# Values of an RWKV-7 layer: one transposed copy of off-head rows, and copies moved from ScalarE to GpSimd and VectorE

## The chip, the cores and the metric

The kernel runs on one core of a Trainium2 chip. Its engines are named as in the profile: PE (TensorE, matrix multiplication and transposes), PEld (its weight loads), DVE (VectorE), ACT (ScalarE), POOL (GpSimd) and SP (SyncE, which here issues the loads of weights). Each engine works through its own instructions in order, and engines wait for each other by semaphores. The metric is the device time of one execution in microseconds; shorter is better.

## The reference

One block of a streaming encoder on 256 tokens of width 2048, in float32: an RMSNorm, one input projection, two mixers in parallel (RWKV-7 with 16 heads of 64, and a latent attention), gates, an output projection, a feed-forward part with a convolution, and a per-layer embedding. The change touches the RWKV-7 recurrence alone. For each head it keeps a 64 x 64 state and runs over the tokens:

```python
def step(state, inp):
    r_t, w_t, k_t, v_t, kk_t, a_t = inp
    sa = jnp.einsum('bhvk,bhk->bhv', state, -kk_t)
    state = (state * w_t[:, :, None, :]
             + sa[..., None] * (kk_t * a_t)[:, :, None, :]
             + v_t[..., None] * k_t[:, :, None, :])
    y_t = jnp.einsum('bhvk,bhk->bhv', state, r_t)
    return state, y_t
```

Before it, r, k and v come out of the projection (mixed with the token before), the decay w and the rate a out of small low-rank products, and kk is the normalised key. After it the output is normalised per head, a bonus term (r k r_k) v is added, and a gate multiplies.

## The kernel before

**The whole.** All weights stream from HBM in pieces of 128 x 1024 float32 (tile `raw`). Each half of a piece is split into a rounded part `hi` (an ACT cast, L148) and a remainder `lo` (a DVE subtraction, L149), and each product is made of three fast matmuls (L183 to L185 in `fm3`: hi by hi, hi by remainder, `lo` by hi). There are 5 buffers each for `hi` and `lo`, and 3 for `raw`. This stream of dense matmuls goes on through the whole kernel.

**The RWKV stage.** Two heads make a pair j: 128 channels on the 128 partitions, head 0 on partitions 0 to 63 and head 1 on 64 to 127. Two pairs run side by side (`par` 0 and 1), and four such double pairs, which this text calls turns, follow each other. `rw_pair` (L714) is a generator that yields between its steps. The loop at L1045 advances the current turn, the prologue of the next one and the epilogue of the last one, and after each step lets the dense work go on by so many matmul groups. In the machine code this makes blocks of 12, 18 or 30 dense matmuls on PE between the steps of the recurrence. A scheduler then sets the order on each engine by priorities and its own estimate of times; that order is fixed when the kernel is built, and each engine keeps to it.

**One turn.** The recurrence is worked in four chunks of 64 tokens.

- *Prologue* (L728 to L808): decays (`ld`, `cs`, `pp`, `pin`), normalised keys (`kk`, whose squares `sq` go to PE at L767 as `pq`), then `kr` (keys and receptances, scaled) and `bk` (columns 0 to 63 the beta keys, 64 to 127 the k' keys, and for head 1 once more the beta keys in 128 to 191, L799, so that each head finds its two blocks side by side).
- *Inverse* (L811 to L904): products `pg` (L820), masked into `gm`, and the inverse of a 64 x 64 triangular matrix per chunk and head: blocks of 16 by substitution on DVE (L848 to L859), then to 32 by two rounds of small matmuls, `ph` and `px` (L889 to L894), then to 64 (L897 to L903). `Y` and `H`, halves of the tile `YH`, hold the transposed inverse and the product between. The finished inverse lies in `Xb`: its two diagonal blocks of 32 are copied per partition quarter by ACT (L914, four copies a pair), the off-diagonal ones come from `px` (L902 on ACT, L903 on DVE).
- *Turned keys* (L906 to L912): `pb` holds the transposed keys of one head, in PSUM, and ACT copies it into `bt`, once per head.
- *Values* (L916 to L930): see below.
- *Chunk loop* (L934 to L955), for each chunk: `pc` = gm by sv (L939); its two heads' blocks are copied into `R` (L940 on ACT, L941 on DVE); Xb by R (L943); the result, negated, goes into the own-head blocks of `av` (L944 on ACT, L945 on DVE); bt by av (L952) and the decayed state `s0` (L949, ACT) give the next chunk's state in `sv` (L954, DVE).
- *Epilogue* (L957 to L999): the outputs `yc` from kb by sv and gm by av, the norm, bonus, gate, and a split into `yrw` (L161, L162).

**How sv and av are laid out.** Both are [128, 4 chunks, 2 halves, 64]. In sv, partitions of head h hold in half h the state of that head (64 key channels by 64 value channels), and in the other half the values of a chunk, turned (64 tokens by 64 value channels). So for head 0 the values stand on partitions 64 to 127, for head 1 on partitions 0 to 63, and one matmul with a 128-row contraction takes state and values in one go. av has the same off-head blocks; its own-head blocks are written in the chunk loop.

Before the change PE transposes v in blocks of 128 tokens that start at tokens 0, 64 and 128, and a fourth from `vw`, a small tile that GpSimd fills with tokens 192 to 255 and 0 to 63 (L784, L785). By this shift both heads' values land on the partitions where they belong, but as pieces that have to be put in place: three ACT copies into sv and the same three into av (L924 to L926), of 64 partitions each. GpSimd clears the two own-head blocks of sv's first chunk (L930).

**Tiles and buffers.** In the RWKV stage `e1` gives tiles of 128 x 256 from 7 buffers per parity, `e2` tiles of 128 x 512 from 3. PSUM has two small buffers per parity (`small`). A tile's first writer waits until the last reader of the tile that held the buffer is done.

Of the kernel before, what the change touches and what calls it, by code (L numbers as in the profile page):

```python
# [12 lines left out]
ALU = mybir.AluOpType  # L13
# [95 lines left out]
def hybrid_block(tc, A):  # L109
# [604 lines left out]
    def rw_pair(J, j, k, r, v):  # L714
# [11 lines left out]
        c4 = lambda ap: ap.rearrange("p (c n) -> p c n", c=NCH)  # L726

# [55 lines left out]
        vw = ep.tile([P, 2, C], F32, name=f"vw{par}", bufs=1)  # L783
        nc.gpsimd.tensor_copy(vw[:, 0, :], v[:, 3 * C:4 * C])  # L784
        nc.gpsimd.tensor_copy(vw[:, 1, :], v[:, 0:C])  # L785
# [13 lines left out]
        act(bk[64:128, :, 2 * C:3 * C], bk[64:128, :, 0:C], AF.Copy)  # L799
# [28 lines left out]
        yield NONE, STEP  # L828

# [41 lines left out]
        heads = ((0, slice(0, 64)), (1, slice(64, 128)))  # L871
# [11 lines left out]
        YH = e2("YH")  # L883
# [6 lines left out]
        tt(out=H, in0=ph, in1=K("lm", 0, 32).unsqueeze(1).to_broadcast([P, NCH, 32]), op=ALU.mult)  # L890
        yield NONE, STEP
        px = each("px", own, lambda i, c: H[Q[i], c, :], Xc)
        tt(out=Xc[:], in0=Xc[:], in1=px, op=ALU.subtract)
        nc.vector.transpose(out=Y, in_=Xc[:])  # L894
# [3 lines left out]
        act(H[Q[1]], ph[Q[1]], AF.Copy)  # L898
        nc.vector.tensor_copy(H[Q[3]], ph[Q[3]])
# [7 lines left out]
        for h in range(2):  # L907
            hs = slice(64 * h, 64 * h + 64)
            pb = small("pb")
            for c in range(NCH):  # L910
                nc.tensor.transpose(pb[:, c * C:c * C + C], bk[hs, c, h * C:h * C + 2 * C], ident[hs, hs])
            act(bt[:, :, h, :], pb[:, 0:T].rearrange("p (c n) -> p c n", c=NCH), AF.Copy)  # L912
        for i in range(4):
            act(Xb[Q[i], :, i // 2, i % 2 * 32:i % 2 * 32 + 32], Xc[Q[i]], AF.Copy)  # L914
# [4 lines left out]
        for c in range(3):  # L919
            nc.tensor.transpose(pv[:, c * P:c * P + P], v[:, c * C:c * C + P], ident)  # L920
        nc.tensor.transpose(pv[:, 3 * P:4 * P], vw[:].rearrange("p a n -> p (a n)"), ident)
        p4 = pv[:].rearrange("p (c n) -> p c n", c=NCH)
        for dst in (sv, av):
            act(dst[0:64, :, 1, :], p4[0:64, :, C:P], AF.Copy)  # L924
            act(dst[64:128, 1:4, 0, :], p4[64:128, 0:3, 0:C], AF.Copy)
            act(dst[64:128, 0, 0, :], p4[64:128, 3, 0:C], AF.Copy)  # L926
        R = ep.tile([P, C], F32, name=f"R{par}", bufs=1)
        lo_, hi_ = slice(0, 64), slice(64, 128)
        for h, hs in heads:
            nc.gpsimd.memset(sv[hs, 0, h, :], 0.0)  # L930
        two = lambda ap: ap.rearrange("p h n -> p (h n)")
# [513 lines left out]
```

## Time and profile before

| | before |
|---|---|
| median of 3 runs | 1575.75 us (1575.26 to 1576.95) |
| the profiled execution | 1574.22 us |
| its span, first to last instruction | 1572.4 us |
| mean granted clock of PE | 0.996 |
| busy in the span: PE, DVE, ACT, POOL | 1544.4, 1178.2, 966.1, 29.7 us |
| the RWKV stage | about 180 to 600 us of the span |

The page gives busy times, a map of the span in 40 slices, the chain of work that ended last, and the costliest groups of instructions. In a group's row stand source line, engine, operation, written and read tiles, shape and count; then busy time and mean; then the idle time of the engine just before these instructions, with what ended it. In the view of waits a row names the engine and line that waited, what released it, the total in us, the number of times and the longest. In the view of stretches a row gives busy time and number of instructions of each engine, the clock that PE was granted (1.00 is full speed), the busy share of the DMA engines, and GB/s. The view of one line gives minimum, median and longest duration in ns. In the timeline a row begins with the start and the duration in us; in square brackets stands the idle time before it.

The clock of PE can be lower than full speed for a few microseconds, and a PE that runs slowly counts as busy all the same. Matmuls overlap, so a row's duration is more than the time that one of them adds.

### The profile page before, as it was taken

How to read it: one execution, taken by the hardware profiler on the slowest of the kernel's cores; microseconds unless marked ns; L12 is line 12 of the kernel's file. 1: busy time of each engine (PE TensorE's matmuls, PEld its weight loads, DVE VectorE, ACT ScalarE, POOL GpSimd, SP SyncE). 2: the span in 40 equal slices, each digit the busy share in tenths (PEclk: the TensorE clock that was granted, in tenths of full speed). 3: DMA queues.
4: the chain of work that ended last, by engine and by line, in shares of the span. 5: the costliest groups of instructions: out<-in, count | busy, mean ns of one | idle time of the engine just before them, and what ended most of it. 6: DMA issues, size and time to landing. Idle time of an engine off the chain costs nothing.

```text
span 1572.4 us, 29627 instructions
## 1 busy us (share of the span) xinstructions
PE 1544.4 (98%) x10850; PEld 1393.2 (89%) x10850; DVE 1178.2 (75%) x2662; ACT 966.1 (61%) x2032; POOL 29.7 (2%) x77
## 2 busy tenths in 40 slices
PE   9999999999999999999999999999999999999997
PEld 9989998999989999887888888888888888888886
DVE  7896786897978866657787777777777656777866
ACT  7686766557575665456765655556565555776653
POOL 0000100000000002000000000000000000000000
PEclk9999999999999999999999999999999999999999
DMA  8654554453444546865656565655555566666564
GB/s 310 183 175 135 164 172 149 134 166 118 138 147 122 174 135 207 285 211 168 194 189 198 190 200 177 203 184 201 183 193 195 167 194 195 199 191 196 165 198 150
DMA packets 80482, 285.19 MB, mean 181 GB/s; under 512 B 9040, under 2 KB 10320, under 8 KB 80336
## 3 DMA queue, kind: packets, MB, share of 16 engines
q1 hardware_dynamic: 77760, 279.48, 55.6%
q10 hardware_dynamic: 2576, 3.81, 0.7%
q8 instruction: 85, 1.39, 0.3%
q14 instruction: 61, 0.50, 0.1%
HBM read 281.16 MB, written 2.10 MB: 180 GB/s over the span
## 4 chain that ended last, share of the span: by engine, by line
PE 85%; DVE 8%; ACT 5%; issue 1%; DMA 1%; DVEq 0%; ACTq 0%
PE d L170 20%; PE d L174 10%; PE d L183 8%; PE d L185 7%; PE d L184 7%; PE o L198 6%; PE o L196 6%; PE o L200 6%; DVE lo L149 3%; PE e L196 2%; PE e L198 2%; PE e L200 2%; ACT hi L148 2%; DMA raw<-in_w_in 1%; DVE pd L858 1%
## 5 line engine op out<-in xcount | busy, mean ns | idle before, releaser
L149 DVE TENSOR_TENSOR lo<-raw,hi 128x512 fp32r<-128x512 f32 x684 | 460.4, 688 | 219.9 <-ACT hi L148 216.1
L148 ACT CAST hi<-raw 128x512 fp32r<-128x512 f32 x684 | 410.9, 619 | 290.1 <-PE o L200 95.8
L183 PE MATMUL d<-uT,hi 128*128 128x256 f32 x1072 | 309.3, 289 | 0.2
L170 PE MATMUL d<-u,highs 128*128 128x512 f32 x1312 | 305.5, 390 | 0.0
L185 PE MATMUL d<-uT,lo 128*128 128x256 f32 x1072 | 301.7, 281 | 0.5 <-DVE lo L149 0.4
L184 PE MATMUL d<-uT,hi 128*128 128x256 f32 x1072 | 301.4, 281 | 0.0
L170 PEld LDWEIGHTS d<-u,highs 128*128 128x128 f32 x1312 | 243.3, 188 | 48.9
L148 ACT CAST highs<-raw 128x512 fp32r<-128x512 f32 x328 | 186.9, 617 | 108.9 <-DMA raw<-in_w_up 84.4
L183 PEld LDWEIGHTS d<-uT,hi 128*128 128x128 f32 x1072 | 203.1, 189 | 2.4 <-ACT hi L161 0.4
L185 PEld LDWEIGHTS d<-uT,lo 128*128 128x128 f32 x1072 | 202.9, 189 | 1.9 <-DVE lo L149 1.2
L184 PEld LDWEIGHTS d<-uT,hi 128*128 128x128 f32 x1072 | 203.2, 190 | 0.1
L149 DVE TENSOR_TENSOR hi<-raw,highs 128x512 fp32r<-128x512 f32 x164 | 112.8, 689 | 78.2 <-PE d L174 61.9
L174 PE MATMUL d<-u,lo 128*128 128x256 f32 x752 | 117.7, 280 | 0.0
L149 DVE TENSOR_TENSOR lo<-raw,highs 128x512 fp32r<-128x512 f32 x164 | 112.1, 685 | 0.0
L174 PE MATMUL d<-u,hi 128*128 128x256 f32 x656 | 103.3, 279 | 0.0
L174 PEld LDWEIGHTS d<-u,lo 128*128 128x128 f32 x752 | 101.7, 188 | 0.8
L174 PEld LDWEIGHTS d<-u,hi 128*128 128x128 f32 x656 | 91.6, 188 | 3.5
L198 PE MATMUL o<-lo,fsplit 128*128 128x512 f32 x264 | 88.6, 390 | 0.0
L196 PE MATMUL o<-hi,fsplit 128*128 128x512 f32 x264 | 88.5, 389 | 0.0
L200 PE MATMUL o<-hi,fsplit 128*128 128x512 f32 x264 | 88.4, 389 | 0.0
L1227 ACT ACTIVATE cy<-d 128x512 f32<-128x512 f32 x44 | 26.3, 597 | 73.3 <-PE d L174 73.3
L198 PEld LDWEIGHTS o<-lo,fsplit 128*128 128x128 f32 x264 | 49.6, 188 | 10.6 <-DVE lo L149 0.3
(395 smaller groups left out, 2550.8 us busy)
## 6 DMA issues: line engine op xcount, KB each, us to landing
raw<-in_w_up SPq DMA_DIRECT2D x176, 512.0 KB, 4.3
raw<-in_w_in SPq DMA_DIRECT2D x133, 512.0 KB, 3.6
raw<-in_w_down SPq DMA_DIRECT2D x88, 512.0 KB, 4.3
raw<-in_w_out SPq DMA_DIRECT2D x32, 512.0 KB, 4.2
raw<-in_w_pg SPq DMA_DIRECT2D x32, 512.0 KB, 3.7
raw<-in_w_bm SPq DMA_DIRECT2D x16, 512.0 KB, 3.8
raw<-in_w_br SPq DMA_DIRECT2D x16, 512.0 KB, 3.7
raw<-in_w_kv SPq DMA_DIRECT2D x8, 512.0 KB, 3.6
```

Of the source, the lines that this page charges most:

```text
L148: nc.scalar.copy(hi[:], raw[:, c:c + 512])
L149: tt(out=lo[:], in0=raw[:, c:c + 512], in1=hi[:].bitcast(F32), op=ALU.subtract)
L170: mm(ps[:, c, :], hi(i, col, P), mov[i][2], start=first and x == 0 and i == 0, stop=False)
L174: mm(ps[:, c, 0:T], lo(i, col, P), mov[i][0], start=False, stop=last and x == len(parts) - 1 and i == len(mov) - 1)
L183: mm(ps[:, c, :], hi(i, col, P), mov[i][:, 0:T], start=f, stop=False)
L184: mm(ps[:, c, :], hi(i, col, P), mov[i][:, T:2 * T], start=False, stop=False)
L185: mm(ps[:, c, :], lo(i, col, P), mov[i][:, 0:T], start=False, stop=l)
L196: mm(b[:], h, hi(i, g * 512, 512), start=f, stop=False)
L198: mm(b[:], h, lo(i, g * 512, 512), start=False, stop=False)
L200: mm(b[:], x, hi(i, g * 512, 512), start=False, stop=l)
L858: tt(out=pd[:, :, 0:t + 1], in0=x8[:, :, 0:t + 1], in1=r8[:, :, 0:t + 1, t], op=ALU.mult)
L1227: act(y[:], ps[:, :, 0:T], AF.Copy)
```

## The change

- *Values.* `vw` becomes a tile [128, 4 chunks, 2, 64] from the `e2` buffers. For each head GpSimd clears the own-head half and copies the head's values into the other half. PE turns each chunk's 128 x 128 block with one transpose, and what comes out has sv's layout, zeros in the own-head blocks included. One ACT copy of 128 x 512 (marked as of high priority) fills sv. GpSimd copies sv into av. The clearing of sv goes.
- *Diagonal blocks of the inverse.* The four copies of Xc into Xb go from ACT to GpSimd, and stand ahead of the last `ph` step.
- *Keys.* The copy of beta keys into bk's third block goes from ACT to GpSimd.
- *bt.* Of its two copies out of PSUM, the second goes from ACT to DVE.
- *Order and buffers.* Five DVE and ACT instructions of the inverse get high priority. `YH`, 128 x 256, moves from the `e2` to the `e1` buffers.

```diff
@@ -724,6 +724,7 @@
             return pss.tile([P, 512], F32, name=nm, tag=f"s{par}")
 
         c4 = lambda ap: ap.rearrange("p (c n) -> p c n", c=NCH)
+        heads = ((0, slice(0, 64)), (1, slice(64, 128)))
 
         lwr = ep.tile([P, 4, P], F32, name="lwr", tag="lwr", bufs=2)
         nc.scalar.dma_start(lwr[:], A["w_lora"][j].rearrange("p (a n) -> p a n", a=4))
@@ -780,9 +781,6 @@
         tt(out=kk[:], in0=kk[:], in1=nr[:, 0:T], op=ALU.mult)
         yield NONE, STEP
         yield HOLD, STEP
-        vw = ep.tile([P, 2, C], F32, name=f"vw{par}", bufs=1)
-        nc.gpsimd.tensor_copy(vw[:, 0, :], v[:, 3 * C:4 * C])
-        nc.gpsimd.tensor_copy(vw[:, 1, :], v[:, 0:C])
         bk = ep.tile([P, NCH, 3 * C], F32, name=f"bk{par}", bufs=1)
         kr = ep.tile([P, NCH, P], F32, name=f"kr{par}", bufs=1)
         tt(out=kr[:, :, 0:C], in0=c4(kk[:]), in1=pp[:, :, 0:C], op=ALU.mult)
@@ -796,7 +794,7 @@
         kp = e1("kp")
         tt(out=kp[:], in0=k, in1=a[:], op=ALU.mult)
         tt(out=bk[:, :, C:2 * C], in0=c4(kp[:]), in1=c4(pin[:]), op=ALU.mult)
-        act(bk[64:128, :, 2 * C:3 * C], bk[64:128, :, 0:C], AF.Copy)
+        nc.gpsimd.tensor_copy(bk[64:128, :, 2 * C:3 * C], bk[64:128, :, 0:C])
         yield NONE, STEP
         rk = e1("rk")
         stt(out=rk[:], in0=r, scalar=V("r_k", j), in1=kp[:], op0=ALU.mult, op1=ALU.mult)
@@ -826,6 +824,11 @@
             act(gm[hs, :, 0, h, :], kr[hs, :, 0:C], AF.Copy)
             nc.gpsimd.tensor_copy(kb[hs, :, h, :], kr[hs, :, C:P])
         yield NONE, STEP
+
+        vw = e2("vw", [P, NCH, 2, C])
+        for h, hs in heads:
+            nc.gpsimd.memset(vw[hs, :, h, :], 0.0)
+            nc.gpsimd.tensor_copy(vw[hs, :, 1 - h, :], c4(v)[hs])
 
         dm = e1("dm", [P, NCH, C])
         b4 = lambda ap: ap.rearrange("p c (b j) -> p c b j", j=16)
@@ -868,7 +871,6 @@
         tt(out=Xc[:].rearrange("p c (b j) -> p c b j", j=16), in0=xc.unsqueeze(2).to_broadcast([P, NCH, 2, 16]),
            in1=K("m32", 0, 2).unsqueeze(1).unsqueeze(3).to_broadcast([P, NCH, 2, 16]), op=ALU.mult)
         yield NONE, STEP
-        heads = ((0, slice(0, 64)), (1, slice(64, 128)))
         cc = lambda p: p[:, 0:T].rearrange("p (c n) -> p c n", c=NCH)
         Q = [slice(32 * i, 32 * i + 32) for i in range(4)]
 
@@ -880,23 +882,28 @@
                     mm(ps[Q[o], 32 * c:32 * c + 32], lhsT(i, c), rhs[Q[i], c, :], start=True, stop=True)
             return ps[:, 0:P].rearrange("p (c n) -> p c n", c=NCH)
 
-        YH = e2("YH")
+        YH = e1("YH")
         Y, H = [YH[:, P * i:P * i + P].rearrange("p (c n) -> p c n", c=NCH) for i in range(2)]
         own = [(i, i) for i in range(4)]
         nc.vector.transpose(out=Y, in_=Xc[:])
         yield AHEAD, STEP
 
         ph = each("ph", own, lambda i, c: n[Q[i], c, i % 2 * 32:i % 2 * 32 + 32], Y)
-        tt(out=H, in0=ph, in1=K("lm", 0, 32).unsqueeze(1).to_broadcast([P, NCH, 32]), op=ALU.mult)
+        with tc.high_priority():
+            tt(out=H, in0=ph, in1=K("lm", 0, 32).unsqueeze(1).to_broadcast([P, NCH, 32]), op=ALU.mult)
         yield NONE, STEP
         px = each("px", own, lambda i, c: H[Q[i], c, :], Xc)
-        tt(out=Xc[:], in0=Xc[:], in1=px, op=ALU.subtract)
-        nc.vector.transpose(out=Y, in_=Xc[:])
+        with tc.high_priority():
+            tt(out=Xc[:], in0=Xc[:], in1=px, op=ALU.subtract)
+            nc.vector.transpose(out=Y, in_=Xc[:])
+        for i in range(4):
+            nc.gpsimd.tensor_copy(Xb[Q[i], :, i // 2, i % 2 * 32:i % 2 * 32 + 32], Xc[Q[i]])
         yield NONE, STEP
 
         ph = each("ph", [(0, 1), (2, 3)], lambda i, c: n[Q[i], c, 32:64], Y)
-        act(H[Q[1]], ph[Q[1]], AF.Copy)
-        nc.vector.tensor_copy(H[Q[3]], ph[Q[3]])
+        with tc.high_priority():
+            act(H[Q[1]], ph[Q[1]], AF.Copy)
+            nc.vector.tensor_copy(H[Q[3]], ph[Q[3]])
         yield NONE, STEP
         px = each("px", [(1, 0), (3, 2)], lambda i, c: H[Q[i], c, :], Xc)
         act(Xb[Q[0], :, 0, 32:64], px[Q[0]], AF.Copy, scale=-1.0)
@@ -909,26 +916,20 @@
             pb = small("pb")
             for c in range(NCH):
                 nc.tensor.transpose(pb[:, c * C:c * C + C], bk[hs, c, h * C:h * C + 2 * C], ident[hs, hs])
-            act(bt[:, :, h, :], pb[:, 0:T].rearrange("p (c n) -> p c n", c=NCH), AF.Copy)
-        for i in range(4):
-            act(Xb[Q[i], :, i // 2, i % 2 * 32:i % 2 * 32 + 32], Xc[Q[i]], AF.Copy)
+            o = pb[:, 0:T].rearrange("p (c n) -> p c n", c=NCH)
+            act(bt[:, :, h, :], o, AF.Copy) if h == 0 else nc.vector.tensor_copy(bt[:, :, h, :], o)
         yield FREE, STEP
         sv = e2("sv", [P, NCH, 2, C])
         av = e2("av", [P, NCH, 2, C])
         pv = small("pv")
-        for c in range(3):
-            nc.tensor.transpose(pv[:, c * P:c * P + P], v[:, c * C:c * C + P], ident)
-        nc.tensor.transpose(pv[:, 3 * P:4 * P], vw[:].rearrange("p a n -> p (a n)"), ident)
-        p4 = pv[:].rearrange("p (c n) -> p c n", c=NCH)
-        for dst in (sv, av):
-            act(dst[0:64, :, 1, :], p4[0:64, :, C:P], AF.Copy)
-            act(dst[64:128, 1:4, 0, :], p4[64:128, 0:3, 0:C], AF.Copy)
-            act(dst[64:128, 0, 0, :], p4[64:128, 3, 0:C], AF.Copy)
+        two = lambda ap: ap.rearrange("p h n -> p (h n)")
+        for c in range(NCH):
+            nc.tensor.transpose(pv[:, c * P:c * P + P], two(vw[:, c]), ident)
+        with tc.high_priority():
+            act(sv[:].rearrange("p c h n -> p (c h n)"), pv[:], AF.Copy)
+        nc.gpsimd.tensor_copy(av[:], sv[:])
         R = ep.tile([P, C], F32, name=f"R{par}", bufs=1)
         lo_, hi_ = slice(0, 64), slice(64, 128)
-        for h, hs in heads:
-            nc.gpsimd.memset(sv[hs, 0, h, :], 0.0)
-        two = lambda ap: ap.rearrange("p h n -> p (h n)")
         yield NONE, STEP
 
         for c in range(NCH):
```

The lines of the changed kernel are numbered anew: L799, L912, L914 and L924 to L926 of before answer to L797, L920, L900 and L929 of the change; L763, L890, L940 and L949 to L764, L893, L941 and L950.

**ACT, second turn, from the turned keys to the first chunk.** Here `pv` is the PSUM tile with the turned values, `kk` and `sq` belong to the next turn's prologue, `z` is an evacuated projection. Before, first the values of the first pair, then the squares:

```order
L148 CAST hi<-raw 128x512
L924 ACTIVATE sv<-pv 64x4x64
L361 ACTIVATE z_4937<-d,omu 128x256
L925 ACTIVATE sv<-pv 64x3x64
L926 ACTIVATE sv<-pv 64x64
L924 ACTIVATE av<-pv 64x4x64
L925 ACTIVATE av<-pv 64x3x64
```

```order
L760 ACTIVATE kk<-z_3273,vec 128x256
L763 ACTIVATE sq_5484<-kk 128x256
L148 CAST hi<-raw 128x512
L763 ACTIVATE sq_5486<-kk 128x256
L940 ACTIVATE R_5433<-pc 64x64
```

Now:

```order
L920 ACTIVATE bt<-pb 128x4x64 x2
L761 ACTIVATE kk<-z_3277,vec 128x256
L764 ACTIVATE sq_5468<-kk 128x256
L764 ACTIVATE sq_5470<-kk 128x256
L148 CAST hi<-raw 128x512
L929 ACTIVATE sv<-pv 128x512 x2
L950 ACTIVATE s_5533<-sv,pp_3889 128x128
L950 ACTIVATE s_5538<-sv,pp_3894 128x128
```

Twelve copies became two, the squares moved from behind the copies to ahead of them, and the evacuation of z stands earlier, outside this piece.

**DVE, second turn, between the first ph and px** (the two yf tiles belong to the epilogue of the turn before). Before:

```order
L890 TENSOR_TENSOR YH_5099<-ph_5119,cst_58 128x128
L149 TENSOR_TENSOR lo_5345<-raw_5342,hi_5344 128x512
L162 TENSOR_TENSOR yrw_2497<-yf_4722,yrw_2497 128x256
L162 TENSOR_TENSOR yrw_2497<-yf_4733,yrw_2497 128x256
L890 TENSOR_TENSOR YH_5101<-ph_5137,cst_58 128x128
```

Now:

```order
L893 TENSOR_TENSOR YH_5095<-ph_5115,cst_58 128x128
L149 TENSOR_TENSOR lo_5349<-raw_5346,hi_5348 128x512
L893 TENSOR_TENSOR YH_5097<-ph_5133,cst_58 128x128
L162 TENSOR_TENSOR yrw_2497<-yf_4718,yrw_2497 128x256
L162 TENSOR_TENSOR yrw_2497<-yf_4729,yrw_2497 128x256
```

The two splits of yrw moved behind the second product; a remainder (L149) still stands between the two.

**POOL, from the second turn's kb copies to the next turn's keys.** Now:

```order
L825 COPY kb_2504<-kr_4252 64x4x64 x2
L825 COPY kb_2505<-kr_4256 64x4x64 x2
L900 COPY Xb_2502<-Xc_5059 32x4x32 x4
L900 COPY Xb_2503<-Xc_5065 32x4x32 x4
L930 COPY av<-sv 128x512 x2
L797 COPY bk_5740<-bk_5740 64x4x64
L797 COPY bk_5744<-bk_5744 64x4x64
```

Before, only the kb copies, the clearing of sv and the short vw copies stood here; the order of PE's instructions is the same but for the transposes' operands and the place of some small matmuls among the dense ones.

## The prediction

> **What bounds the kernel now.** I read the page's busy shares first, then the stretches of the RWKV stage, then who TensorE waits for in it. In the rows with a colon the columns are stretch, length, busy time of PE, PEld, DVE, ACT and POOL, granted clock, DMA share and GB/s.
>
> ```profile
> PE 1544.4 (98%) x10850; PEld 1393.2 (89%) x10850; DVE 1178.2 (75%) x2662; ACT 966.1 (61%) x2032; POOL 29.7 (2%) x77
> ...
> 180.00:600.00 420.00, 406.85 (x4365) 395.35 (x4364) 334.60 (x1041) 265.58 (x640) 18.45 (x61) 0.99 0.48 147
> 256.00:280.00 24.00, 20.98 (x228) 19.57 (x227) 13.25 (x36) 21.64 (x64) 1.40 (x4) 1.00 0.32 101
> 310.00:348.00 38.00, 38.00 (x415) 37.20 (x415) 36.88 (x137) 20.59 (x42) 0.00 (x0) 1.00 0.49 152
> 348.00:380.00 32.00, 28.33 (x340) 26.91 (x338) 19.74 (x60) 25.38 (x73) 1.01 (x4) 0.95 0.42 131
> 448.00:476.00 28.00, 25.70 (x267) 25.07 (x266) 16.92 (x54) 22.56 (x67) 0.97 (x4) 0.94 0.39 115
> 540.00:562.00 22.00, 20.52 (x291) 19.53 (x290) 11.35 (x27) 17.40 (x49) 0.00 (x0) 1.00 0.49 147
> ```
>
> TensorE is the bound: it is busy 98% of the span, so only its idle time can be won. The change lies wholly in the stage from 180 to 600, where TensorE idles 420 - 406.85 = 13.15 us. The four short stretches are those where the four turns go from the inverse into the chunk loop; they hold 3.02 + 3.67 + 2.30 + 1.48 = 10.5 us of it. ACT is the crowded engine there (21.64 of 24 in the first); in the inverse (310 to 348) DVE is nearly full, yet TensorE loses nothing. The waits of TensorE from 184 to 600, as total, times and longest:
>
> ```profile
> PE pq L767 <- ACT sq L763: 3.7, 3, 2.3
> PE pc L939 <- issue: 3.2, 2, 2.0
> PE px L880 <- DVE YH L890: 2.8, 4, 1.3
> PE pc L943 <- DVE R L941: 1.0, 1, 1.0
> PE pc L939 <- DVE sv L954: 0.7, 2, 0.6
> ```
>
> The "issue" of the second row is a wait for ACT too: the timeline of the first turn shows the last of its sv copies ending at 274.27 + 0.21 = 274.48, and TensorE going on at 274.57.
>
> ```profile
> 274.27 0.21 ACT L926 ACTIVATE sv<-pv 64x64 f32<-64x64 f32 x1
> ...
> 274.57 0.46 PE L939 MATMUL pc<-sv,gm 128*128 128x128 f32 x2 [1.96 <-issue]
> ...
> 368.01 0.46 PE L939 MATMUL pc<-sv,gm 128*128 128x128 f32 x2 [1.24 <-issue]
> ...
> 370.65 0.61 PE L767 MATMUL pq<-cst,sq 128*128 128x2 f32 x4 [1.00 <-ACT sq L763]
> ```
>
> The idle time has a second price, in the clock column. In the second turn, after the waits of 1.24 and 1.00 us of the last two rows above:
>
> ```profile
> 372.00:373.00 1.00, 1.00 (x8) 1.00 (x7) 0.91 (x6) 0.20 (x2) 0.00 (x0) 0.64 0.00 0
> 373.00:374.00 1.00, 1.00 (x7) 1.00 (x6) 0.72 (x4) 0.48 (x1) 0.00 (x0) 0.50 0.87 98
> 374.00:375.00 1.00, 1.00 (x7) 1.00 (x7) 0.50 (x3) 0.73 (x3) 0.00 (x0) 0.50 0.82 336
> 375.00:376.00 1.00, 1.00 (x7) 1.00 (x7) 0.93 (x8) 0.00 (x0) 0.00 (x0) 0.65 0.23 90
> ```
>
> TensorE counts as busy here but runs at half clock: 0.36 + 0.50 + 0.50 + 0.35 = 1.71 us lost. The third turn has one more, after its wait of 2.3: 0.06 x 28 = 1.7 us by the row of 448 to 476. Together 3.4 us; the first and fourth turns show clock 1.00.
>
> [...]
>
> **The change part by part.** First, ACT. Of its groups in 184 to 600, L914, L924 to L926 and L799 go and L912 halves; L354, L361 and L763 are here for their means (behind the bar: the idle time before them):
>
> ```profile
> L914 ACT ACTIVATE Xb<-Xc 32x128 f32<-32x128 f32 x32 | 9.8, 307 | 2.8 <-DVE Xc L893 2.5
> ...
> L361 ACT ACTIVATE z<-d,omu 128x256 f32<-128x256 f32 x16 | 7.5, 471 | 8.2 <-DVE z L362 8.0
> ...
> L912 ACT ACTIVATE bt<-pb 128x256 f32<-128x256 f32 x16 | 4.8, 384 | 0.5 <-PE pb L911 0.5
> L354 ACT ACTIVATE mix<-d 128x512 f32<-128x512 f32 x8 | 4.7, 589 | 0.0
> ...
> L799 ACT ACTIVATE bk<-bk 64x256 f32<-64x256 f32 x8 | 3.3, 416 | 1.6 <-DVE bk L793 1.3
> ...
> L763 ACT ACTIVATE sq<-kk 128x256 f32<-128x256 f32 x8 | 3.1, 410 | 0.0
> ...
> L924 ACT ACTIVATE sv<-pv 64x256 f32<-64x256 f32 x8 | 3.0, 377 | 0.6 <-PE pv L921 0.6
> L924 ACT ACTIVATE av<-pv 64x256 f32<-64x256 f32 x8 | 3.0, 376 | 0.2
> ...
> L925 ACT ACTIVATE sv<-pv 64x192 f32<-64x192 f32 x8 | 2.6, 326 | 0.1
> ...
> L926 ACT ACTIVATE sv<-pv 64x64 f32<-64x64 f32 x8 | 1.7, 210 | 0.0
> ```
>
> The av copies of L925 and L926 cost as those of sv, so the twelve copies of a turn make 7.3 x 2 / 4 = 3.65 us. Off ACT: 9.8 + 2.4 + 3.3 + 14.6 = 30.1 us. Onto it: eight copies of 128x512 out of PSUM, which L354 has at 0.589, 4.7 us. Net 25 us, 6.3 a turn.
>
> What counts is how much earlier the second pair's sv is there. Ahead of it went, in a turn: two bt copies (0.77), the first av (0.91), and 1.83 us of sv copies, now 1.18. Two z evacuations (0.94) move ahead of the crowded place; two squares (0.82) move into it. That is 0.77 + 0.91 + 0.65 + 0.94 - 0.82 = 2.45 us, and up to 2.46 more for the eight Xb copies, part of which only filled time before px. The lateness was 1.24 and 1.96 us. So the 3.2 us of pc go, with 0.5 us of margin in the first turn at worst. The squares now stand ahead of sv instead of behind twelve copies: the 3.7 us of pq go. The 1.0 us of R in the fourth turn had L940 queued behind the av copies: gone too. Sum 7.9 us.
>
> Second, the order on DVE. In the second turn the two splits of L162 stood between the two L890; now they follow them.
>
> ```profile
> 350.36 0.76 DVE L162 TENSOR_TENSOR yrw<-yf,yrw 128x256 fp32r<-128x256 f32 x2
> ```
>
> So 0.76 of the 1.3 us wait goes. In the other turns the rows around L890 keep their order (a cast's remainder, L149, still stands between), so 1.5 us of L890 stays, as does L954 (0.7).
>
> Third, the clock. Without the clusters of waits both dips go: 3.4 us. TensorE's own work doesn't change: four transposes a pair before and after.
>
> Fourth, what DVE and GpSimd get. DVE: eight copies of 128x256 from PSUM; L808, which reads a PSUM tile of that size, is the nearest row. GpSimd: its rows, and the DVE row that shows how it is met (minimum, median, longest, in ns):
>
> ```profile
> L808 DVE TENSOR_TENSOR bo<-z,pr 128x256 f32<-128x256 f32 x8 | 3.2, 416 | 0.1
> ...
> L785 POOL COPY vw<-z x8: 230/241/718, 183.0 to 459.7; 128x64 f32<-128x64 f32 x8
> ...
> L827 POOL COPY kb<-kr x16: 390/448/929, 190.3 to 498.5; 64x256 f32<-64x256 f32 x16
> ...
> L149 DVE TENSOR_TENSOR lo<-raw,hi x684: 650/691/789, 9.4 to 1545.3; 128x512 fp32r<-128x512 f32 x171
> ```
>
> The bt copies are 3.3 us in stretches where DVE is busy 13.25 of 24 and 19.74 of 32: hidden, 0 us; 3.3 if that room is gone. For GpSimd I estimate from 241 ns for 64 elements and 448 for 256: 0.30 for an Xb copy, 0.72 for 128x512. A pair gets two vw copies in place of two short ones (+0.41), bk (0.45), four Xb (1.2) and av (0.72): 2.8 us, 22 us in all. None is awaited at once. Xb's eight copies of a turn (2.4 us) start with the final Xc and are needed only at L943, behind the px, pb and pv steps. av must be written before L944 overwrites a block of it: two copies end 1.44 us after the first sv, while TensorE reaches L943 at sv + 0.59 + 18 dense matmuls at 0.092 us (415 in 38 us), 2.2 us. One stretched as the longest L827 (+0.48) still fits. On GpSimd's queue the next turn's bk and vw stand behind av, but their readers are a chunk loop away.
>
> What GpSimd can take is DVE's time. The longest L149 is 0.10 us over its median while GpSimd's copies grew by 0.48: GpSimd mostly gives way. Eighty copies at 0.10 are 8 us on DVE; TensorE waits on DVE for 4.5 of its 13.15 us (L890, R and L954), so most of these 8 us meet no wait; I take 1.0 us, a judgement. The ends are 0, and all 22 us.
>
> [...]
>
> **The sum.** The profiled execution took 1574.22 us (its span 1572.4). 1574.22 - 7.9 - 0.76 - 3.4 + 1.0 = 1563.2. The median of the runs, 1575.75, lies 1.53 above it: **1564.7 us**.
>
> **The rivals.** *Still late, or still gated*: the first turn's margin of 0.5 us is eaten, or a similar wait of about 2 us appears, and with it one dip of 1.7: 1564.7 + 3.7 = 1568.4. Near it, 1568.1, lies the case that both dips have another cause than the waits and stay. For it speak ACT at 90% there and the first turn, whose 1.96 us brought no dip; against it the 2.46 us that I left out, and that both dips follow directly on the waits.
>
> *DVE holds the turns*: the waits return one step later, at px and pc, because DVE is 36.88 of 38 full in the inverse; only the fourth turn's 1.0 us stays won: about 1574.7, no change. Against it: DVE idled along with TensorE in the crowded stretches (13.25 of 24), so its work simply starts earlier.
>
> *GpSimd takes DVE's time*: the one that ends slower. Its place is L149, whose lo every dense matmul group awaits; its price is the 22 us of copies plus 3.3 of bt. It decides once more than 12 of these 25 us reach TensorE; all of them give 1575.75 - 12.1 + 25.5 = 1589. For it: full DVE stretches. Against: most copies fall where DVE is half idle, and the 0.10 us of L149.
>
> *More than forecast*: the kept 1.5 + 0.6 + 0.7 us also go, and GpSimd costs nothing: 1564.7 - 3.8 = 1560.9.
>
> **How the numbers follow.** Forecast 0.60 (1561.5 to 1567.5), still late or gated 0.15, more 0.07, DVE holds 0.11, slower 0.07. The range 1560 to 1572 takes in the first three, 0.82. About 0.2% (3.15 us) is what a measurement of this kernel can tell from no change; below 1572.6 lie the same three: faster 0.82, same 0.11, slower 0.07.
>
> **What would show it.** In the changed profile: no row of TensorE waiting for L763 or for sv above 0.3 us; clock 1.00 in all four stretches; TensorE idle of 4 to 5 us in place of 13.15 in the stage; ACT's busy time down by some 25 us, DVE's up by 3 to 10; GpSimd near 50 to 60 us. I am wrong if a wait of TensorE on lo (L149) or on av or Xb comes up with more than 2 us, if L149's mean grows by over 0.02 us, or if a dip of the clock stays.

## The result, and the profile after

The changed kernel takes 1560.62 us (median of 5 runs, 1560.34 to 1561.42); the kernel before, on the same chip, 1575.75. The ratio is 0.9907 (95% interval 0.9894 to 0.9921). That is 15.1 us faster where 11.0 were forecast; the forecast of 1564.7 is 4.1 us too high. The time lies in the range of 1560 to 1572, but near its lower end, below the forecast's own band (1561.5 to 1567.5) and beside the rival *more than forecast* (1560.9, chance 0.07). The runs' times are medians of fast executions; one execution of a later run, `xb_act`, took 3097.65 us and is left out. The profiled execution took 1560.39 us, its span 1558.6 (before: 1572.4, so 13.8 less).

The busy shares and the RWKV stage of the changed kernel. The stage now ends some 14 us earlier (the last matmul of `pgt` starts at 582.5 us, before at 596.3), so the row of stretches is given up to 590 too:

```profile
PE 1538.0 (99%) x10850; PEld 1388.3 (89%) x10850; DVE 1182.2 (76%) x2670; ACT 942.1 (60%) x1944; POOL 60.9 (4%) x125
...
180.00:600.00 420.00, 415.20 (x4481) 405.30 (x4480) 347.60 (x1063) 248.63 (x565) 52.90 (x111) 1.00 0.50 155
180.00:590.00 410.00, 405.20 (x4396) 395.30 (x4395) 341.37 (x1052) 242.75 (x554) 50.33 (x110) 1.00 0.49 153
256.00:280.00 24.00, 23.73 (x260) 22.94 (x259) 17.98 (x56) 19.33 (x52) 4.42 (x10) 1.00 0.42 130
344.00:376.00 32.00, 31.54 (x388) 30.72 (x387) 24.71 (x76) 22.18 (x58) 4.41 (x10) 1.00 0.49 153
440.00:470.00 30.00, 30.00 (x318) 29.42 (x317) 23.62 (x72) 20.71 (x55) 3.96 (x9) 1.00 0.45 139
530.00:556.00 26.00, 26.00 (x285) 25.45 (x284) 14.77 (x36) 15.80 (x38) 3.78 (x10) 1.00 0.50 159
```

The last four rows are the places where the turns go from the inverse into the chunk loop. TensorE idles 0.27 + 0.46 + 0 + 0 us there instead of 10.5, and its clock is 1.00 in each. In the whole stage it idles 410 - 405.20 = 4.80 us instead of 13.15. What is left, in the view of TensorE's waits in the stage:

```profile
PE pc L940 <- DVE sv L955: 1.9, 4, 0.9
PE px L882 <- DVE YH L893: 1.7, 4, 0.6
PE pw L740 <- DVE lws L735: 0.4, 1, 0.4
PE pc L944 <- DVE R L942: 0.3, 1, 0.3
```

Nothing in it waits for ACT any more. In the first turn, where TensorE had waited 1.96 us for the last sv copy, the timeline of the changed kernel has the second pair's copy end at 267.68 + 1.09 = 268.77, and TensorE come to the first product of the chunk loop at 271.42:

```profile
267.68 1.09 ACT L929 ACTIVATE sv<-pv 128x512 f32<-128x512 f32 x2
...
271.42 0.61 PE L940 MATMUL pc<-sv,gm 128*128 128x128 f32 x4
```

What the moved copies cost, by groups of lines (184 to 590):

```profile
L900 POOL COPY Xb<-Xc 32x128 f32<-32x128 f32 x32 | 13.1, 408 | 180.7 <-DVE Xc L897 179.4
L930 POOL COPY av<-sv 128x512 f32<-128x512 f32 x8 | 4.7, 610 | 28.7 <-ACT sv L929 28.7
```

And the view of the line L149, with minimum, median and longest duration in ns over the whole span:

```profile
L149 DVE TENSOR_TENSOR lo<-raw,hi x684: 648/691/887, 9.6 to 1530.7; 128x512 fp32r<-128x512 f32 x171
```

GpSimd is 31.2 us busier over the span, VectorE 4.0. Of these, 3.1 are its bt copies by the view of groups (eight rows of 0.42, which overlap a little), which leaves 0.9 us that GpSimd can have taken from it.

### The profile page after: what moved, and what is told of

Its sections match the earlier page's. It is cut to its first block, busy times and chain, and to the rows that moved or that the text cites. A ratio compares the mean times of both kernels' runs of the same rounds, so it can differ in the third digit from the quotient of the medians.

```text
span 1558.6 us, 29636 instructions
## 1 busy us (share of the span) xinstructions
PE 1538.0 (99%) x10850; PEld 1388.3 (89%) x10850; DVE 1182.2 (76%) x2670; ACT 942.1 (60%) x1944; POOL 60.9 (4%) x125
## 4 chain that ended last, share of the span: by engine, by line
PE 89%; DVE 6%; ACT 2%; DMA 1%; issue 1%; DVEq 0%; ACTq 0%
PE d L170 21%; PE d L174 11%; PE d L183 9%; PE d L185 8%; PE d L184 8%; PE o L196 7%; PE o L198 6%; PE o L200 6%; PE e L196 2%; PE e L198 2%; PE e L200 2%; DVE lo L149 2%; ACT hi L148 1%; DMA raw<-in_w_in 1%; PE tr L237 0%
## 5 line engine op out<-in xcount | busy, mean ns | idle before, releaser
L149 DVE TENSOR_TENSOR lo<-raw,hi 128x512 fp32r<-128x512 f32 x684 | 461.0, 690 | 213.9 <-ACT hi L148 208.5
L149 DVE TENSOR_TENSOR hi<-raw,highs 128x512 fp32r<-128x512 f32 x164 | 112.7, 688 | 76.8 <-PE d L174 58.8
L149 DVE TENSOR_TENSOR lo<-raw,highs 128x512 fp32r<-128x512 f32 x164 | 112.0, 684 | 0.0
```

The lines of the kernel that those rows point to most:

```text
L149: tt(out=lo[:], in0=raw[:, c:c + 512], in1=hi[:].bitcast(F32), op=ALU.subtract)
```

## The experiments

All kernels were timed in five rounds against the kernel before on the same chip. The theory under test is the forecast's: TensorE waited for a crowded ACT, the two half-clock dips hang on those waits, and GpSimd takes next to nothing. Its rivals are that GpSimd takes VectorE's time, and that parts of the change do nothing. One number for each run, its difference to the kernel before beside it, is best read with an uncertainty of about 2 us (that is what the intervals of the ratios come to); runs that share a chip are compared more closely.

### One half of the change at a time

Run `values` is the kernel before with only the new layout of vw, sv and av; Xb, bk and bt stay on ACT and nothing has priority.

```diff
+        vw = e2("vw", [P, NCH, 2, C])
+        for h, hs in heads:
+            nc.gpsimd.memset(vw[hs, :, h, :], 0.0)
+            nc.gpsimd.tensor_copy(vw[hs, :, 1 - h, :], c4(v)[hs])
...
+        act(sv[:].rearrange("p c h n -> p (c h n)"), pv[:], AF.Copy)
+        nc.gpsimd.tensor_copy(av[:], sv[:])
-        for dst in (sv, av):
-            act(dst[0:64, :, 1, :], p4[0:64, :, C:P], AF.Copy)
...
```

> Only the values part of the change: vw by head in the e2 buffers, sv in one ACT copy, av by GpSimd (and YH in the e1 buffers, which makes room). Xb, bk and bt stay on ACT as before, no priorities in the inverse. If ACT's queue ahead of sv is the cause, as I hold: the squares no longer stand behind twelve copies, so the 3.7 us of pq and the 1.0 us of R go, most of the 3.2 us of pc goes, both clock dips (3.4 us) go: 1563 to 1567 us, about two thirds to three quarters of the gain. If the order on DVE and the lighter inverse are the cause: 1571 or more.

Measured: 1564.62 us (1563.69 to 1565.9), ratio 0.9931 (0.9918 to 0.9945), 10.5 us faster. Run `rest` is the opposite: the changed kernel with the values as they were before.

```diff
-        nc.gpsimd.tensor_copy(av[:], sv[:])
+        for dst in (sv, av):
+            act(dst[0:64, :, 1, :], p4[0:64, :, C:P], AF.Copy)
...
```

> Everything but the values part: Xb and bk copied by GpSimd, half of bt by DVE, the priorities, YH in e1; twelve ACT copies per turn for sv and av as before. By my theory ACT is up to 3.2 us earlier at sv, so the pc waits shrink from 3.2 us to under 1, but the squares still stand behind the copies: pq waits of 1 to 3 us and perhaps one clock dip stay: 1567 to 1571 us. By the rival (order and the inverse): 1562 to 1565.

Measured: 1564.4 us (1563.39 to 1566.54), ratio 0.9932 (0.9919 to 0.9944), 10.8 us faster. TensorE's waits in the stage, first of `values`, then of `rest`:

```profile
PE px L882 <- DVE YH L893: 2.9, 4, 1.5
PE pc L939 <- DVE sv L954: 1.8, 5, 0.7
PE ph L882 <- DVE YH L898: 1.1, 3, 0.7
```

```profile
PE px L880 <- DVE YH L891: 1.7, 4, 0.5
PE pc L943 <- DVE sv L958: 1.5, 4, 0.7
PE pc L947 <- DVE R L945: 1.3, 2, 1.0
PE pq L768 <- ACT av L930: 1.1, 2, 0.7
```

In both the waits of 1.24, 1.96 and 2.3 us are gone, and in both the clock is 1.00 through the whole stage. The expectation for `rest` missed by 2.6 us: I had thought that the twelve copies of the values were needed for the lateness. They are not. Relieving ACT ahead of sv by either half is enough for the long waits and both dips. For `values`, which has no priorities, that is shown. For `rest` it is in part argued: its 1564.4 lies in the range of the rival (order and the inverse, 1562 to 1565), and no run has its relief of ACT without its priorities; against the rival stands that the priorities alone are worth some 2 us (`no_prio`, below) and change only waits for YH. So the two gains, 10.5 and 10.8, overlap, and together they make 15.1. What the second half adds are short waits: `rest` keeps 1.1 us of pq behind the twelve copies, and `values`, which lacks the order on VectorE, keeps 2.9 + 1.1 us of YH.

### One part taken away from the change

Each of these is the changed kernel with one part undone: av by a second ACT copy out of PSUM; without the priorities; Xb, the second bt copy or bk back on ACT.

```diff
-        nc.gpsimd.tensor_copy(av[:], sv[:])                       # av_act
+        act(av[:].rearrange("p c h n -> p (c h n)"), pv[:], AF.Copy)
-        with tc.high_priority():                                  # no_prio, three places
+        if True:
-            nc.gpsimd.tensor_copy(Xb[Q[i], ...], Xc[Q[i]])        # xb_act
+            act(Xb[Q[i], ...], Xc[Q[i]], AF.Copy)                 #   behind the bt copies
-            act(bt[:, :, h, :], o, AF.Copy) if h == 0 else nc.vector.tensor_copy(bt[:, :, h, :], o)
+            act(bt[:, :, h, :], o, AF.Copy)                       # bt_act
-        nc.gpsimd.tensor_copy(bk[64:128, :, 2 * C:3 * C], ...)    # bk_act
+        act(bk[64:128, :, 2 * C:3 * C], ..., AF.Copy)
```

> The changed kernel, but av filled by a second ACT copy of 128x512 from PSUM (two more of 0.59 us per turn) instead of GpSimd. If my worked margin of 0.5 us in the first turn is right, the second pair's sv comes 0.6 us later and costs 0 to 0.5 us there, and nothing in the other turns: 1560.5 to 1562. If GpSimd's taking over of av carries a large part of the gain: 1564 or more.

> The changed kernel without the priorities in the inverse (H, Xc, its transpose, the 32-row copies). The two splits of L162 should stand again between the two products of the second turn, so the waits of px grow by 0.8 us by my sum; 'values', which had no priorities either, shows 2.9 us of px and 1.1 us of ph against 1.7 and none in the changed kernel, which makes 2.3 us: 1561.4 to 1563. If ACT's queue is all there is: 1560.6.

> The changed kernel with the diagonal copies of the inverse on ACT again, in the old place (eight of 0.31 us per turn). Since either half of the change alone took both clock dips away, ACT should still be in time at sv: 1560.6 to 1562.5, with pc or pq waits under 1 us in sum. If the Xb copies are what frees ACT: pc waits of 1 us a turn come back and 1564 or more.

> The changed kernel with both bt copies on ACT (two of 0.37 us per turn back from DVE). DVE has room there and ACT too: within 1 us, 1560 to 1561.6, and by nothing more if the cost of bt on DVE is hidden as I took it (0).

> The changed kernel with the keys' copy (0.42 us, two a turn) on ACT again. GpSimd then copies nothing in the chunk loop, where the run with further copies showed DVE held up (L149 from 0.69 to 1.09 us during a copy). If the two copies a turn cost what those did (0.19 us each reaching the end), this kernel is 1.5 us faster: 1559. If not: 1560.6, as ACT has room.

| run | us (lowest to highest) | ratio to before (95%) |
|---|---|---|
| the change | 1560.62 (1560.34 to 1561.42) | 0.9907 (0.9894 to 0.9921) |
| av_act | 1561.76 (1560.69 to 1562.42) | 0.9913 (0.9900 to 0.9927) |
| no_prio | 1562.39 (1561.7 to 1564.05) | 0.9925 (0.9913 to 0.9937) |
| xb_act | 1563.54 (1562.49 to 1564.76) | 0.9933 (0.9920 to 0.9946) |
| bt_act | 1561.73 (1561.17 to 1562.9) | 0.9921 (0.9908 to 0.9934) |
| bk_act | 1560.37 (1559.59 to 1560.65) | 0.9911 (0.9898 to 0.9923) |

The last four ran on one chip, without the change itself; bk_act, 0.25 us from the change's time on another chip, stands in for it. Against bk_act, Xb on GpSimd is worth 3.2 us, the priorities 2.0 and bt on VectorE 1.4; every execution of these three is slower than every one of bk_act, though the intervals of the ratios overlap. For av (run on another chip) 1.1 us can't be told from nothing, and for bk on GpSimd no gain or cost shows. The expectations held for av_act, no_prio and bk_act (as if the copy cost nothing). `xb_act` missed: 1563.54 is 1.0 us above the 1562.5 that ACT in time at sv would give, while the waits of pc that were to come back did not grow (1.9 us as in the change). `bt_act` is 0.1 us above its range. No kernel of them has a dip in the stage. The waits name the cause in two cases. Without the priorities the wait for the product H is back at its old size (2.8 us as before, where the change has 1.7):

```profile
PE px L882 <- DVE YH L893: 2.8, 4, 1.2
PE pc L940 <- DVE sv L955: 1.9, 4, 0.9
```

With Xb on ACT the next product and the off-diagonal block come later instead (0.9 and 0.6 us; in the change the first has no row and the second 0.2), which names 1.3 of the 3.2 us:

```profile
PE px L882 <- DVE YH L904: 0.9, 2, 0.4
PE pb L916 <- DVE Xb L908: 0.6, 1, 0.6
```

For bt the rows are those of the change; only TensorE's modelled busy time differs (1539.2 against 1538.0), so where its 1.4 us arise stays open.

### What a GpSimd copy costs, in three places

The forecast's least secure term was GpSimd's hold on VectorE. Three kernels add 96 copies of 128 x 512 to the change, SBUF to SBUF, into a tile that nobody reads: in the chunk loop and ahead of the inverse (`pool_more`, in bursts of six), in the inverse (`pool_inv`, twelve a pair), and behind the RWKV stage (`pool_ffn`, eight bursts of twelve).

```diff
+    gsb = ep.tile([P, 512], F32, name="gsb")
...
+        for _ in range(6):                       # pool_more: twice a pair
+            nc.gpsimd.tensor_copy(gsb[:], kr[:].rearrange("p c n -> p (c n)"))
...
+        for _ in range(12):                      # pool_inv: once a pair, behind kb and vw
+            nc.gpsimd.tensor_copy(gsb[:], gm[:, :, 0, :, :])
...
+                if c == 0 and nch[0] in [240 + 34 * x for x in range(8)]:     # pool_ffn
+                    nc.gpsimd.tensor_copy(gsb[:], lo[:].bitcast(F32))
+                    for x in range(11):
+                        nc.gpsimd.tensor_copy(gsb[:], cst[:, 0:512])
```

> The changed kernel with 96 further GpSimd copies of 128x512 (24 a turn, read from kr into a scratch tile that nobody reads, placed after the keys and after kb, in the chunk loop and the inverse where DVE is fullest): GpSimd busy some 60 us more. If GpSimd mostly gives way, as my sum has it (0.10 us of DVE for a copy, a fifth of it reaching TensorE): 1 to 3 us more, 1561 to 1564. If a GpSimd copy takes DVE's time in full, as the slower rival has it: 15 us or more, 1575 and above.

> The changed kernel with the same 96 added GpSimd copies of 128x512 into a tile that nobody reads (nothing is left out), but in the inverse, 12 a pair, ahead of the Xb copies, where VectorE is nearly full and TensorE lost nothing; in the run before they stood in the chunk loop and cost 17.9 us, 0.19 us each. If what costs is that two particular steps of VectorE in the chunk loop are late (the place decides), the same copies cost under 4 us here: 1561 to 1565, and the rows of TensorE's waits stay near those of the changed kernel (pc for sv 1.9 us, px for YH 1.7). If any time that GpSimd takes from a full VectorE reaches TensorE, they cost as much as there: 1573 to 1580, with VectorE 15 to 25 us busier. A third case: the Xb copies queue behind them and come late, which would show as a wait of TensorE for Xb of more than 2 us a turn, 1565 to 1575. L149's mean rises above 690 ns in each.

> The changed kernel with the same number of added GpSimd copies (96 of 128x512, SBUF to SBUF, into a tile that nobody reads; nothing is left out), in 8 bursts of 12 behind the RWKV stage, in the last half of the program, where TensorE has no idle time and VectorE is busy some three quarters of it (105.95 of 140 us). In the chunk loop and in the inverse, where VectorE is nearly full, 96 such copies cost 18 us. If the price is set by how full VectorE is, the time that the copies take from it fits into its idle quarter: 0 to 2 us over the changed kernel, 1560.5 to 1562.5, although L149 beside the bursts is stretched from 0.69 to about 1.05 us. If a GpSimd copy costs some 0.19 us wherever it stands, 1577 to 1580. A case between, 1563 to 1568, would say that a burst holds up more lo tiles than TensorE has in hand (five).

Measured: `pool_more` 1578.52 us (1577.87 to 1580.69), ratio 1.0024 (1.0015 to 1.0033); `pool_inv` 1579.36 (1578.7 to 1580.13), 1.0033 (1.0021 to 1.0046); `pool_ffn` 1562.97 (1562.31 to 1563.68), 0.9917 (0.9903 to 0.9930). Against the change (on another chip) 96 copies cost 17.9 us, 18.7 us and 2.3 us: the whole gain and more in the first two places (1 to 3 us by the sum's price), and in the third little, which the intervals of the ratios don't tell from nothing (the expectation ended 0.5 us below it). In the first two a part is the clock: in the stage of the profiled executions it dips once in `pool_inv` (0.50 at 434 to 436 us, some 1.7 us lost) and for twice as long in `pool_more` (0.50 at 398 to 404 us).

My first reading of `pool_more` was that two steps of the chunk loop were late. The waits of TensorE there spoke for it:

```profile
PE pc L945 <- DVE sv L960: 8.1, 11, 2.5
PE pc L958 <- DVE av L951: 1.8, 2, 1.1
```

`pool_inv` fells that reading. There the chunk loop waits as in the change (1.9 us), TensorE waits for the remainders instead, and the price is the same. Its waits:

```profile
PE d L185 <- DVE lo L149: 8.8, 11, 2.4
PE pc L943 <- DVE sv L958: 1.9, 4, 0.9
```

Two stretches of its second turn, VectorE in the third column of busy times and GpSimd in the fifth:

```profile
320.00:330.00 10.00, 10.00 (x109) 9.80 (x108) 9.92 (x39) 4.76 (x10) 9.26 (x13) 1.00 0.35 105
330.00:340.00 10.00, 7.70 (x59) 6.89 (x59) 9.66 (x30) 4.63 (x11) 7.44 (x10) 1.00 0.48 136
```

VectorE is full while the copies run, and some 10 us after they began TensorE has used up the lo tiles that it had in hand: it loses 2.30 us in the second stretch.

`pool_ffn` shows what the two places have in common. Its copies take even more of VectorE's time: 1210.1 us busy, 27.9 above the change (`pool_more` 20.6, `pool_inv` 18.1). But there VectorE has time to give. A stretch ahead of a burst, and one in it:

```profile
1347.00:1357.00 10.00, 10.00 (x46) 8.29 (x45) 7.64 (x16) 6.94 (x15) 0.23 (x1) 1.00 0.62 186
1357.00:1367.00 10.00, 10.00 (x46) 8.29 (x45) 9.70 (x12) 7.07 (x16) 9.32 (x12) 1.00 0.51 168
```

VectorE's timeline, two rows of each:

```profile
1351.86 0.69 DVE L150 TENSOR_TENSOR lo<-raw,hi 128x512 fp32r<-128x512 f32 x1 [0.33 <-ACT hi L149]
1352.47 0.42 DVE L167 TENSOR_TENSOR fsplit<-f,fsplit 128x256 fp32r<-128x256 f32 x1
...
1358.67 1.10 DVE L150 TENSOR_TENSOR lo<-raw,hi 128x512 fp32r<-128x512 f32 x1
1359.69 0.83 DVE L167 TENSOR_TENSOR fsplit<-f,fsplit 128x256 fp32r<-128x256 f32 x1
```

(L150 and L167 are the change's L149 and L162 in that kernel.) VectorE goes from 7.64 to 9.70 of 10 us, its pauses vanish, and TensorE, with lo tiles in hand, stays at 10.00. The one wait that is new behind the stage is 1.5 us long, beside the last burst, where TensorE needs the result of a single VectorE instruction at once:

```profile
1459.11 0.44 PE L242 MATMUL tr<-cst,h 128*128 128x128 f32 x2 [1.52 <-DVE h L1180]
```

So the price of one of these copies is some 0.2 to 0.3 us of VectorE's time (18.1, 20.6 and 27.9 us for 96), and what reaches TensorE is what VectorE has no idle time for. Where VectorE is full, as in the two stretches of `pool_inv`, nearly all of it does (18.1 us of VectorE's time and 18.7 us of the kernel's, dip included). The rival of the prediction that ends slower has the right mechanism, then, and it can turn this kernel slower than before. The stretched rows (0.69 to 1.10 us, 0.42 to 0.83 us) show VectorE's loss; that the price can vanish into idle time only `pool_ffn` shows (27.9 us of VectorE's time, 2.3 us of the kernel's).

The change's own copies don't keep out of the full stretches. In its second turn Xb, av and vw fall into these three, in this order (VectorE in the third column of busy times, GpSimd in the fifth):

```profile
350.00:352.00 2.00, 2.00 (x42) 1.83 (x38) 1.86 (x5) 1.93 (x7) 1.81 (x4) 1.00 0.51 197
358.00:360.00 2.00, 2.00 (x20) 2.00 (x19) 0.42 (x1) 1.91 (x5) 1.17 (x2) 1.00 0.52 199
384.00:386.00 2.00, 1.37 (x12) 1.17 (x11) 1.97 (x5) 0.62 (x1) 1.78 (x6) 1.00 0.57 170
```

Only av runs where VectorE idles. Beside vw a remainder is stretched (as is the product of the keys ahead of it, L796, 0.62 us where it takes 0.42 in `rest`), and the chunk loop's longest wait for sv follows:

```profile
384.65 0.88 DVE L149 TENSOR_TENSOR lo<-raw,hi 128x512 fp32r<-128x512 f32 x1
386.27 0.46 PE L940 MATMUL pc<-sv,gm 128*128 128x128 f32 x2 [0.90 <-DVE sv L955]
```

In `rest`, where GpSimd copies nothing beside the same steps:

```profile
387.24 0.69 DVE L149 TENSOR_TENSOR lo<-raw,hi 128x512 fp32r<-128x512 f32 x1
388.67 0.46 PE L943 MATMUL pc<-sv,gm 128*128 128x128 f32 x2 [0.52 <-DVE sv L958]
```

So here the change's copies cost TensorE about 0.4 us. Over the whole span they take little of VectorE's time (0.9 us) and are themselves stretched: those of bk take 0.84 us on average, where a copy of that size takes 0.39 at its shortest. Why these short copies of 32 or 64 partitions take so much less than the bursts do, no run shows.

### The waits that are left

Run `a_act` takes a VectorE step of 0.41 us, eight times, out of the chunk loop. `chain_prio` does so too and gives priority to the state's own steps.

```diff
-        ts(out=a[:], in0=a[:], scalar1=V("k_a", j), scalar2=oka[:, j:j + 1], op0=ALU.mult, op1=ALU.add)
+        act(a[:], a[:], AF.Identity, scale=V("k_a", j), bias=oka[:, j:j + 1])
...
+            with tc.high_priority():             # chain_prio: R, av, and the update of sv
                 act(R[lo_, :], o(0, 0, lo_), AF.Copy)
```

> The changed kernel with the scale and offset of a (by k_a) on ACT in place of VectorE: eight instructions of about 0.40 us leave VectorE's chunk loop and eight of about 0.47 us join ACT's (3.8 us, into an engine that is busy 60% of the span). If the waits that the change left (pc for sv 1.9 us, px for YH 1.7) come from VectorE's queue, part of them goes: 1558.5 to 1560.3. If they come from the length of the dependent chain itself, nothing changes: 1560 to 1561.5. If ACT's relief was what made the change faster, and ACT is still near its limit there, waits of TensorE for ACT come back: 1562 or more.

> The run with a on ACT, and the steps of the chunk loop's state (R, av, and the update of sv, on ACT and VectorE) given priority over other work that is ready. If the wait of pc for sv (1.9 us in four places) comes from other VectorE work that stands ahead of the update of sv, it falls below 0.7 us: 1558 to 1560. If the update is already issued as soon as its inputs are there, the wait stays at 1.5 to 2 us and the time with it: 1560 to 1561.5. Slower (1562 or more) if what is put behind them is itself awaited by TensorE (a longer wait for YH, Xb or lo).

Measured: `a_act` 1560.26 us (1559.77 to 1560.72), ratio 0.9912 (0.9898 to 0.9925); `chain_prio` 1558.58 (1557.75 to 1560.08), ratio 0.9900 (0.9884 to 0.9915). The wait of pc for sv falls from 1.9 to 1.0 us in the first, and is gone from the rows of the second, while the wait for YH stays. TensorE's waits in `chain_prio`:

```profile
PE px L882 <- DVE YH L893: 1.8, 4, 0.7
PE ph L882 <- DVE YH L898: 0.6, 1, 0.6
PE pw L740 <- issue: 0.3, 1, 0.3
```

So the kept wait for sv did come from other VectorE work ahead of it. Against `a_act` on the same chip `chain_prio` gains 1.7 us, against the change (another chip) 2.0, with intervals that overlap: it is the fastest kernel here by its median, but not shown to beat the change.

## Why the prediction was right, and where its sizes were off

**The bound and the waits for ACT** (-7.9 us forecast). Right: none of the rows for L763, "issue" or R in the fourth turn is left, and ACT's relief did it, as `values` shows and `rest` bears out. The margin was worked out too carefully. In the first turn the sum was 2.45 us earlier against 1.96 late, "0.5 us of margin at worst", with up to 2.46 more left out for Xb; measured, sv is there 271.42 - 268.77 = 2.65 us before TensorE comes. That part of the 2.46 left out made the difference is likely, but no run gives it alone.

**The clock** (-3.4). Right for the profiled executions, and the first rival's case of dips with another cause is gone: in the stage they vanish with either half, and one comes back with a wait of 2.44 us in `pool_inv`. How many dips an execution has varies, though. The kernel before took 1571.08 us in an execution with a mean clock of 0.998 and 1577.67 in one at 0.994, on one chip; the profiled one had 0.996. The changed kernel's lie at 0.996 to 0.998. By estimate one dip, 1.7 of 1572 us, is 0.001 of the mean clock.

**The order on VectorE** (-0.76). Right in kind, and somewhat larger: the wait for H went from 2.8 to 1.7 us, and without the priorities it is 2.8 again.

**GpSimd** (+1.0). This was called a judgement, and its size is about right: VectorE lost some 0.9 us to GpSimd, not 8, and 0.4 us of it is seen to reach TensorE. Both reasons given were wrong, so the size was partly luck. That TensorE waits on VectorE for only 4.5 us, so that most of a loss meets no wait, doesn't follow: in `pool_inv` VectorE's losses made new waits, where TensorE had lost nothing before. And the copies don't fall mostly where VectorE is half idle, as the rival's "against" had it: beside Xb it is 1.86 of 2 us busy, beside vw 1.97. GpSimd's own time was taken too low, 22 us against 31.2: Xb and bk are stretched (13.1 and 6.7 us where 9.6 and 3.6 were summed), and the clearing of vw (4.9 us against 2.3 for that of sv) was left out. **bt on VectorE** (0): `bt_act` is 1.4 us slower than bk_act, so it may gain a little.

**The size.** The forecast gain is 11.06 us; the span fell by 13.8. All of it lies in the stage: its first landmark (L663) starts at 180.2 before and 180.1 after, its last at 596.3 and 582.5. Recorded idle time there fell by 13.15 - 4.80 = 8.35 us against 7.9 + 0.76 - 1.0 = 7.66 in the sum, the dips by 3.4 as forecast. That leaves 13.8 - 8.35 - 3.4 = 2.05 us that no row of idle time shows. The step that was mis-sized is the use of the waits' rows as a stall's whole price. The timeline of `pool_inv` shows what such a row leaves out:

```profile
331.56 0.28 PE L183 MATMUL d<-uT,hi 128*128 128x256 f32 x1
331.68 0.28 PE L184 MATMUL d<-uT,hi 128*128 128x256 f32 x1
332.48 0.38 PE L185 MATMUL d<-uT,lo 128*128 128x256 f32 x1 [0.52 <-DVE lo L149]
332.70 0.28 PE L183 MATMUL d<-uT,hi 128*128 128x256 f32 x1
332.82 0.28 PE L184 MATMUL d<-uT,hi 128*128 128x256 f32 x1
```

Dense matmuls start every 0.12 us though each row lasts 0.28. From 331.68 to 332.70 pass 1.02 us for two of them, 0.78 more than 0.24; the row calls 0.52 of it idle. So 0.26 us of a stall stand as busy time, and by these rows a stall of less than 0.28 - 0.12 = 0.16 us doesn't show at all. The listed waits of TensorE in the stage fell from 17 to 11: 6 x 0.26 = 1.6 us by estimate, as one stall's figure stands for all. That the last 0.5 are stalls too short for a row is argued, not shown; in `pool_inv`, whose stage is 19.0 us longer, 10.5 of it idle and 1.7 a dip, the same count (26 waits against 11) covers 3.9 of the 6.8 us left. The times differ by 15.1 - 13.8 = 1.3 us more: the profiled execution of the kernel before is 1.53 us faster than its median, about one dip. The sum had carried this difference over to the changed kernel, whose profiled execution is only 0.23 us below its median. The rival that the time came nearest to, *more than forecast*, didn't come about: the kept waits for YH and sv were to go, and they are 1.7 + 1.9 us. So the path was right, and the size was off by what the sum had no terms for.

**The signs.** Held: no wait for L763, clock 1.00, idle 4.80 (4 to 5 forecast), ACT 24.0 us less busy (25), VectorE 4.0 more (3 to 10), GpSimd 60.9 (50 to 60, just above). None of the signs of being wrong came: L149's mean is 0.690 us against 0.688. Not held: sv was to stay below 0.3 us, and pc waits 1.9 us for it, 0.9 at the longest. That is another wait than the one meant, for VectorE's update between chunks (L955), which stood at 0.7 before; 0.4 us of the growth is VectorE's work stretched beside vw, and `chain_prio` shows that other VectorE work stands ahead of it.

## What to carry to other kernels

Work out by how much the last producer is late, not how many copies stand ahead of it: two reliefs that each suffice don't add, and the second one pays only in what comes next. A burst of copies given to GpSimd is paid for in VectorE's time (0.2 to 0.3 us for a 128 x 512 copy here), so put it where VectorE idles by the view of stretches, and price it in full where VectorE is 9.9 of 10 us busy, whether or not TensorE waits there yet; short single copies cost much less here (0.9 us of VectorE's time for all of the change's). Add to each stall in a row of TensorE's waits what the overlap of matmuls hides, 0.26 us in the one measured here, and read the granted clock of several executions before a dip is priced from one.

## What the runs showed of the hardware

- **A dip of the clock can follow a wait of 1.76 us, and the length of the wait alone doesn't decide it.** In the stage, waits of 2.3 us (third turn before), of 1.24 and 1.00 us within 3.9 us (second turn) and of 2.44 us (`pool_inv`) were each followed by a stretch at half clock; one of 1.96 us (first turn before) was not. Ahead of the stage, some 93 us into the span, every kernel here has a wait for ScalarE of 1.68 to 1.85 us. In `values` and `bk_act` it is equally long; the clock falls in the first only:

```profile
93.24 0.58 PE L196 MATMUL dv<-hi,latm 128*128 128x512 f32 x1 [1.76 <-ACT zs L354]
94.00:96.00 2.00, 2.00 (x6) 1.56 (x5) 1.92 (x5) 1.95 (x5) 0.00 (x0) 0.50 0.64 229
```

```profile
92.97 0.50 PE L196 MATMUL dv<-hi,latm 128*128 128x512 f32 x1 [1.76 <-ACT zs L354]
94.00:96.00 2.00, 2.00 (x10) 1.64 (x9) 1.92 (x5) 1.97 (x5) 0.00 (x0) 1.00 0.58 227
```

  It also falls there in `xb_act` and `pool_more` (1.84), `pool_ffn` (1.77) and `a_act` (1.78), and doesn't in `av_act` (1.84) or `pool_inv` (1.85). What decides between equal waits, no run shows.
- **GpSimd's copies and VectorE's subtractions stretch each other.** VectorE's 128 x 512 subtraction goes from 0.69 to 1.10 us, its 128 x 256 one from 0.42 to 0.83 (`pool_ffn`); in `pool_inv` the products of the substitution (L864) go from 286 to 358 ns on average, the reductions between them (L865) stay (225, in the change 227); GpSimd's 128 x 512 copy takes 0.61 us beside an idling VectorE (av) and 0.78 on average in `pool_inv`.
